# Layer-0 experts ranked by token count on the chip: ten places of 128 slots, six of 64 in pairs

## The chip, the cores and the metric

One core of a Trainium2 chip runs the whole kernel in one launch. The metric is the device time of an execution in microseconds, the median of several runs; a profiled execution gives the trace.

## The reference

A two-layer diffusion block on 512 tokens (256 of context, 256 latent) of width 1024. Each layer has a token mixer (an mLSTM, latent attention and a gated MLP side by side) and then a mixture of 16 experts. Only the experts of layer 0 matter here. A router picks for each token one of four groups and in it two experts, with weights:

```python
combine = einsum('blk,blke->ble', top_w, one_hot(expert_id, 16))
out = zeros_like(h)
for e in range(16):
    hidden = silu(h @ w1[e]) * (h @ w3[e])      # 1024 x 512 each
    out = out + combine[..., e:e+1] * (hidden @ w2[e])   # 512 x 1024
```

All is float32. In layer 0 all 512 tokens go through it, so 1024 pairs of a token and an expert, 64 for an expert on average; in the last layer only the 256 latent tokens.

## The kernel before, in words

`block_kernel` (L1724) runs mixer 0, the layer-0 experts, mixer 1, the layer-1 experts and the last norm. The weights (6.29 MB for an expert, float32) stream from memory once.

`stream_rows` (L1677) makes the plan of the layer-0 weights. It walks the experts 0 to 15; for each it adds the k-steps of w1 and w3 in turn (`("h", e, w)`, eight each; a k-step is a row of 128 x 512, 256 KB), and behind them the eight of w2 of the expert before (`("y", e - 1, q)`). `Pipe.add` (L112) cuts this into units by the tag of the buffer that takes each: FIRST0 (L52) for the first 29 units, then RING0 (L53) round and round, 16 units of 28 rows. There are 221 units. A unit is one DMA on SP's queue (L158), issued as soon as its buffer is free; units 0 to 18 (`PRE0`, 40 rows: both first matrices of experts 0 and 1 and the second of expert 0) are loaded before the router (L1820).

`Pipe.fill` (L162) splits each unit, three items ahead of use, into a rounded half (ACT, L99) and the rest (DVE, a few on POOL, L100), both in the format fp32r. `mm3` (L84) then does three matmuls for each product (L85 to L87), hi x hi, hi x lo and lo x hi.

`route` (L1142) writes the normalized tokens to memory (`h2d`), makes the logits, and ranks each token among those of its expert (`rp`; `pr[:, nt]` holds the counts). Its `weights` (L1241) makes the combine weights `wE` and the largest count `mci`. All of that is small work on DVE.

`moe_rows` (L1340) gives each expert 128 slots. `slots` (L1351) makes one-hot tiles (slot against token) and from them the row index `idx`; `gather` (L1387) is an indirect DMA on POOL that fetches the token rows; `prep` (L1392) transposes them and splits them; `slot_weights` (L1372) brings the combine weight to the slots. The loop over the experts (L1475) issues the gather of e + 3, prepares e + 1, makes slots of e + 4, then does the two first products of e (48 matmuls), SiLU (L1495), the product with the other half (L1498), and the second product of e - 1 (24 matmuls, `second`, L1411), whose result ACT scales and an indirect DMA on POOL adds into `fsum` in memory (L1427). The last two experts (`LATE`) stay on the chip and are added by matmul. At e = 4 (`OVER0`) every engine loads the largest count into a register (L1500) and branches: over 128, a slow loop over all experts would add the tokens beyond (`overflow`, L1316); the profiled execution does not take it.

`moe_chip` (L1531), the experts of layer 1, works in pairs: two experts share a tile of 128 slots, 64 each. Their weights are used unsplit; each product is two matmuls of 64 columns, one for each half of the slots (L1641, L1592), read by `paired` (L1666), which takes a unit of the one and one of the other.

Buffers that matter: `a` (nine: gathered tokens, x, ysb, split tiles), `h` (8), `b2` (6), `w`, `wa`, `e2` (2 each), `t2` (4).

Of the kernel before, what the change touches and what calls it, by code (L numbers as in the profile page):

```python
# [21 lines left out]
P = 128  # L22
D = 1024
KT = 8
# [31 lines left out]
TURN = 8  # L56
OVER0 = 4
EARLY1 = ((0, 1), (14, 15), (16, 17), (), (), (), ())
WHO = ("01010101", "0101")
# [43 lines left out]
class Pipe:  # L103
# [8 lines left out]
    def add(self, key, parts, kt, nk, kind=""):  # L112

        tag = self.tags(len(self.units))
        nk = min(unit_rows(tag), nk)
        u = len(self.units)
        self.units.append((tag, [p[kt * P:(kt + nk) * P] for p in parts], nk))
# [1024 lines left out]
def route(g, l):  # L1142
# [98 lines left out]
    def weights():  # L1241
        r.rk = rk = sm("rk", [P, 5, 16])
        nc.vector.tensor_copy(rk[:, 0:nt + 1], pr[:, 0:nt + 1])
        mc = sm("mc", [P, 1])
        nc.vector.tensor_reduce(mc, rk[:, nt, :], axis=AX.X, op=ALU.max)
        r.mci = g.s([P, 1], I32, "mci")
# [20 lines left out]
        for k, dst in ((0, r.wE), (1, w2)):  # L1267
            nc.vector.tensor_tensor(dst, Ek[:, k, 0:nt].rearrange("p t a b -> p t (a b)"), pw[:, :, k:k + 1].to_broadcast([P, nt, 16]), op=ALU.mult)
        nc.vector.tensor_tensor(r.wE, r.wE, w2, op=ALU.add)
    r.weights = weights  # L1270
    return r
# [44 lines left out]
def overflow(g, l, r, cap, put_tile):  # L1316
# [3 lines left out]
    wt = g.s([P, 4, 16], F32, "ovw")  # L1320
    nc.vector.tensor_scalar(wt[:, 0:nt], r.rk[:, 0:nt], float(cap) - 0.5, None, op0=ALU.is_gt)
    nc.vector.tensor_tensor(wt[:, 0:nt], wt[:, 0:nt], r.wE, op=ALU.mult)
# [16 lines left out]

def moe_rows(g, r, st, cap=P):  # L1340

    nc = g.nc
    nt = r.nt
    n_tok = nt * P
    idx = g.s([P, 16, 1], I32, "idx")
    sw = g.s([P, 16], F32, "sw")
    wp = g.s([P, 4, 16, 3], BF16, "wp")
# [3 lines left out]
    def slots(e):  # L1351
# [3 lines left out]
        for i in range(nt):  # L1355
            oh = g.s([P, P], BF16, "oh")
            ohs.append(oh)
            nc.vector.tensor_scalar(oh, g.iota, r.rp[:, i, e:e + 1], None, op0=ALU.is_equal)
# [4 lines left out]
        if e >= NE - LATE:  # L1363
            tok = g.s([P, 1], F32, "tok")
# [7 lines left out]
    def slot_weights(e, ohs):  # L1372
        pt = g.mm()[:, 0:3]
        for i in range(nt):
            nc.tensor.matmul(pt, ohs[i], wp[:, i, e, :], start=(i == 0), stop=(i == nt - 1))
        nc.vector.tensor_reduce(sw[:, e:e + 1], pt, axis=AX.X, op=ALU.add)

    def weight_planes():

        rest = g.s([P, 4, 16], F32, "rest")  # L1380
        nc.vector.tensor_copy(wp[:, :, :, 0], r.wE)
        nc.vector.tensor_tensor(rest, r.wE, wp[:, :, :, 0], op=ALU.subtract)
        nc.vector.tensor_copy(wp[:, :, :, 1], rest)
        nc.vector.tensor_tensor(wp[:, :, :, 2], rest, wp[:, :, :, 1], op=ALU.subtract)
# [7 lines left out]
    def prep(e):  # L1392
        x = g.t([P, 2, KT, P], F32R, "a", "x")
        for q in range(2):
            pt = g.bank([P, 4, P], "pt")
            for c in range(4):
                k = q * 4 + c
                nc.tensor.transpose(pt[:, c, :], xg[(e // 2) % 2][:, e % 2, k * P:(k + 1) * P], g.ident)
            split_from(g, x[:, 0, q * 4:q * 4 + 4, :], x[:, 1, q * 4:q * 4 + 4, :], pt)
        return x  # L1400

    def turned(G):

        pt = g.bank([P, 4, P], "pt")
        for c in range(4):
            nc.tensor.transpose(pt[:, c, :], G[:, c * P:(c + 1) * P], g.ident)
        gh, gl = [g.t([P, 4, P], F32R, "cz", "gtr") for _ in range(2)]
        split_from(g, gh, gl, pt)
        return gh, gl

    def second(e, gh, gl):  # L1411
        ysb = g.t([P, 2, D], F32R, "a", "yhl") if e in late else g.t([P, D], F32, "a", "ysb")
        for q in range(2):
            py = g.bank([P, 512], "py")
            for kt, nk, raw in st.matrix(("y", e, q), 4):
                for kk in range(nk):
# [9 lines left out]
        if e not in late:  # L1426
            nc.gpsimd.indirect_dma_start(out=g.fsum, out_offset=bass.IndirectOffsetOnAxis(ap=idx[:, e, 0:1], axis=0),  # L1427
                                         in_=ysb, in_offset=None, bounds_check=n_tok - 1, oob_is_err=False, compute_op=ALU.add)
        return last
# [14 lines left out]
    def total(k, e, ps):  # L1444

        y, C = late[e]
        for part in range(2):
            nc.tensor.matmul(ps, y[:, part, k * P:(k + 1) * P], C, start=(e == NE - LATE and part == 0), stop=(e == NE - 1 and part == 1))

# [24 lines left out]
    pend = None  # L1474
    for e in range(NE):  # L1475
        if e + 3 < NE:
            gather(e + 3)
        if e + 1 < NE:
            xs[e + 1] = prep(e + 1)
        if e + 4 < NE:  # L1480
            slot_weights(e + 4, slots(e + 4))
        x = xs.pop(e)
        ph = [g.mm() for _ in range(2)]
        at = [0, 0]
        while min(at) < KT:
            if pend is not None and len(pend) == 2 and sum(at) >= TURN:
                pend = (pend[0],) + turned(pend[1])
            w = st.peek()[2]
# [6 lines left out]
        last = nc.scalar.activation(G, ph[0], AF.Silu)  # L1495
        if e == NE - 1:
            preload(g, last, AF.Sqrt)
        nc.vector.tensor_tensor(G, G, ph[1], op=ALU.mult)  # L1498
        if e == OVER0:
            cnt = nc.values_load(r.mci[0:1, 0:1], min_val=0, max_val=T)  # L1500
            with g.tc.If(cnt > cap):
                def put(i, acc):
                    for q in range(2):
# [4 lines left out]
                        nc.sync.dma_start(rows, acc[q])  # L1508
                overflow(g, 0, r, cap, put)
        if pend is not None:  # L1510
            last = second(*pend)
            if e == NE - LATE:
                fs = load_sums()
        pend = (e, G)
    ps = {k: g.mm() for k in range(4)}
    for k in range(4):
        total(k, NE - 2, ps[k])
    second(pend[0], *turned(pend[1]))
    with g.tc.issue_after(last.ins):
        for k in range(KT):  # L1520
            add_sums(k)
    for k in range(KT):
        if k >= 4:
            ps[k] = g.bank([P, 512], "tot")
            total(k, NE - 2, ps[k])
        total(k, NE - 1, ps[k])
        to_x(k, ps[k], WHO1[k] == "1")
# [149 lines left out]
def stream_rows(g):  # L1677
# [3 lines left out]

    def ys(e):
        for q in range(2):
            st.add_matrix(("y", e, q), [w2_view(g, 0, e, q)], 4)
    for e in range(NE):
        at = [0, 0]
        while min(at) < KT:
            w = 0 if at[0] <= at[1] else 1
            at[w] += st.add(("h", e, w), [(g.e_w1, g.e_w3)[w][0, e]], at[w], KT - at[w])
        if e:  # L1690
            ys(e - 1)
    ys(NE - 1)
    return st
# [30 lines left out]
def block_kernel(ctx, tc, x_t, c_t, vecs, w_ada, w_adt, w_in, w_gk, w_uq2, a_wukv, gws, gbs, w_pa, w_pb, w_pc, w_out,  # L1724
# [56 lines left out]
    g.w4 = const("w4", [P, 4])  # L1781
    nc.gpsimd.iota(g.w4, [[-1, 4]], base=4, channel_multiplier=0, allow_small_or_imprecise_dtypes=True)

    g.mask = [const(f"mask{d}", [P, P], dt=BF16) for d in range(2)]
# [156 lines left out]
```

## Time and profile before

| | |
|---|---|
| median of 3 runs | 1627.12 us (1625.97 to 1627.9) |
| the profiled execution | 1623.76 us |
| its span | 1622.0 us |
| TensorE busy | 1516.7 us, 94% |
| VectorE busy | 1079.6 us, 67% |
| ScalarE busy | 709.6 us, 44% |
| moved by DMA | 358.25 MB, mean 221 GB/s |
| mean granted TensorE clock | 0.974 |

The span runs from the first to the last instruction. The layer-0 experts take the stretch from about 650 to 962 us, the layer-1 experts from about 1360 on. A share of a whole span mixes stages with different limits; the stretch of the change has rows of its own below. A busy TensorE is not TensorE at its peak, since the ends of matmuls are modelled and overlap.

### The profile page before, as it was taken

To read this page: it belongs to the slowest core of one execution; us is meant where nothing else is said; L and a number is where in the kernel's file an instruction comes from. 1 tells how busy PE (TensorE), PEld (TensorE's weight loads), DVE (VectorE), ACT (ScalarE), POOL (GpSimd) and SP (SyncE) were. 2 spreads that over 40 slices of the span, in tenths; PEclk is the share of its full clock that TensorE was granted. 3 is DMA by queue.
4 is the path that set the end of the run, shared out by engine and by line. 5 is a ranking of instruction groups with operands and counts; after the bars stand their busy time and mean duration, and the time that the engine had idled before them with its cause. 6 is when DMAs were issued, how large, how long until landed. Compare 5 with 4: busy or idle time off the path is not lost. (4 is left out here: it accounts for less than half of the span.)

```text
span 1622.0 us, 22586 instructions
## 1 busy us (share of the span) xinstructions
PE 1516.7 (94%) x8283; PEld 1136.6 (70%) x8283; DVE 1079.6 (67%) x2085; ACT 709.6 (44%) x1185; POOL 131.3 (8%) x129
## 2 busy tenths in 40 slices
PE   7899999997999997898979999999999998999997
PEld 5677777686777776676867776886789996453443
DVE  4868996488987655887968977576587675222213
ACT  3335333444422322676867776534566452011011
POOL 1001000003000022211211111010020001000000
PEclk9999999998999999999999999999999999999999
DMA  9615464123477884598999992422236786899995
GB/s 320 209 51 189 156 195 129 40 66 117 148 246 263 276 290 165 185 298 271 357 317 296 367 341 65 124 82 78 65 103 187 254 277 228 320 386 387 386 386 218
DMA packets 180969, 358.25 MB, mean 221 GB/s; under 512 B 13934, under 2 KB 30894, under 8 KB 180592
## 3 DMA queue, kind: packets, MB, share of 16 engines
q1 hardware_dynamic: 173920, 341.10, 62.0%
q0 software_dynamic: 6640, 15.53, 3.6%
q8 instruction: 68, 1.11, 0.3%
q14 instruction: 53, 0.43, 0.1%
q10 hardware_dynamic: 288, 0.07, 0.0%
HBM read 351.77 MB, written 12.60 MB: 225 GB/s over the span
## 5 line engine op out<-in xcount | busy, mean ns | idle before, releaser
L99 ACT ACTIVATE whi<-wraw 128x512 fp32r<-128x512 f32 (+4 forms) x358 | 279.9, 803 | 327.6 <-PE mm L86 220.8
L100 DVE TENSOR_TENSOR wlo<-wraw,whi 128x512 fp32r<-128x512 f32 (+4 forms) x356 | 319.4, 911 | 126.4 <-ACT whi L99 119.1
L85 PE MATMUL mm<-h,whi 128*128 128x512 f32 (+1 forms) x672 | 237.1, 359 | 7.7 <-DVE bt L936 4.0
L86 PE MATMUL mm<-h,whi 128*128 128x512 f32 (+1 forms) x672 | 238.0, 355 | 0.0
L87 PE MATMUL mm<-h,wlo 128*128 128x512 f32 (+1 forms) x672 | 233.3, 352 | 2.1 <-DVE wlo L100 2.1
L85 PEld LDWEIGHTS mm<-h,whi 128*128 128x128 f32 x672 | 129.4, 194 | 31.9 <-DVE bt L936 6.8
L87 PEld LDWEIGHTS mm<-h,wlo 128*128 128x128 f32 x672 | 128.8, 192 | 21.1 <-DVE wlo L100 3.6
L86 PEld LDWEIGHTS mm<-h,whi 128*128 128x128 f32 x672 | 129.6, 193 | 18.6 <-issue 4.4
L100 DVE TENSOR_TENSOR whl<-wraw,whl 128x1024 fp32r<-128x1024 f32 (+1 forms) x110 | 115.0, 1068 | 15.2 <-ACT whl L99 15.2
L1641 PE MATMUL mm<-wraw,x 128*64 128x512 f32 x504 | 121.2, 596 | 0.0
L335 DVE CUSTOM_DVE_ANT_0 adw<-adw,cbc,vec 128x1024 f32<-128x1024 f32 x80 | 102.1, 1280 | 24.6 <-DMA adw<-in_w_adt 24.2
L99 ACT ACTIVATE whl<-wraw 128x1024 fp32r<-128x1024 f32 (+1 forms) x112 | 100.9, 931 | 21.0 <-issue 9.4
L1641 PEld LDWEIGHTS mm<-wraw,x 128*64 128x64 f32 x504 | 36.7, 137 | 67.5 <-issue 62.7
L85 PE MATMUL mm<-by,whi 128*128 128x512 f32 (+1 forms) x192 | 66.6, 347 | 4.5 <-ACT sg L922 4.5
L87 PE MATMUL mm<-by,wlo 128*128 128x512 f32 (+1 forms) x192 | 65.8, 342 | 0.0
L86 PE MATMUL mm<-by,whi 128*128 128x512 f32 (+1 forms) x192 | 65.7, 342 | 0.0
L86 PE MATMUL mm<-wlo,h 128*128 128x512 f32 x160 | 65.7, 410 | 0.0
L85 PE MATMUL mm<-whi,h 128*128 128x512 f32 x160 | 65.2, 411 | 0.1
L335 DVE CUSTOM_DVE_ANT_0 prod<-adw,cbc,vec 128x1024 bf16<-128x1024 f32 x48 | 61.2, 1280 | 6.0 <-DMA adw<-in_w_adt 5.9
L87 PE MATMUL mm<-whi,h 128*128 128x512 f32 x160 | 64.5, 403 | 0.0
L1592 PE MATMUL py<-wraw,gt 128*64 128x512 f32 x256 | 63.8, 598 | 0.7 <-ACT gt L1582 0.7
L85 PE MATMUL mm<-whi,x 128*128 128x512 f32 x128 | 53.0, 415 | 9.0 <-ACT whi L99 8.8
(455 smaller groups left out, 2971.0 us busy)
## 6 DMA issues: line engine op xcount, KB each, us to landing
wraw<-in_e_w SPq DMA_DIRECT2D x278, 512.0 KB, 8.7
wraw<-in_w_in SPq DMA_DIRECT2D x96, 512.0 KB, 3.9
adw<-in_w_adt SPq DMA_DIRECT2D x80, 512.0 KB, 4.2
wraw<-in_e_w SPq DMA_DIRECT2D x33, 1024.0 KB, 13.2
wraw<-in_e_w SPq DMA_DIRECT2D x76, 256.0 KB, 6.7
adw<-in_w_ada SPq DMA_DIRECT2D x8, 1024.0 KB, 12.3
wraw<-in_w_out SPq DMA_DIRECT2D x16, 512.0 KB, 5.7
wraw<-in_w_pb SPq DMA_DIRECT2D x8, 512.0 KB, 3.6
```

The lines of the kernel that those rows point to most:

```text
L85: nc.tensor.matmul(ps, lh, rh, start=first, stop=False)
L86: nc.tensor.matmul(ps, lh, rl, start=False, stop=False)
L87: return nc.tensor.matmul(ps, ll, rh, start=False, stop=last)
L99: g.nc.scalar.activation(hi, src, AF.Copy)
L100: (eng or g.nc.vector).tensor_tensor(lo, src, hi.bitcast(F32), op=ALU.subtract)
L335: g.nc.vector.tensor_tensor_reduce(out=out, in0=raw, in1=g.cbc[:, s, :], scale=1.0, scalar=g.vec[l][:, C_BADA + j:C_BADA + j + 1], op0=ALU ...
L1592: nc.tensor.matmul(py[hs, :], gt[:, k, hs], raws[s][:, kk, :], start=(k == 0), stop=(k == 3))
L1641: nc.tensor.matmul(ph[w][hs, :], x[:, k, hs], raws[s][:, kk, :], start=(k == 0), stop=(k == KT - 1))
```

## The change

Layer 0 gets 16 places instead of 16 experts. Experts 0 and 1 keep places 0 and 1 (`FIXED`); the others are ranked by token count on the chip (`order`, on DVE) and take places 2 to 15, largest first. Places 0 to 9 (`WIDE`) work as before: 128 slots, split weights, three matmuls for a product. Places 10 to 15 work in three pairs of 64 slots with unsplit weights, as layer 1 does. `ORDER` is the order of these 13 steps. `ordered` permutes the ranks (`rP`) and the combine weights (`wP`) into the order of places. SP loads the numbers of the 14 experts at places 2 to 15 into registers, and the transfers of their weights take their addresses from these. A pair's results are added by two scatters, since both experts may have the same token: the first of the lower 64 slots, the second of all 128 with the lower half out of bounds (`upper`). The branch now asks for a count above the place's own capacity, 128 or 64. The plan has 221 units as before, of the same sizes.

```diff
+FIXED = 2
+WIDE = 10
+ORDER = ((0,), (1,), (10, 11), (2,), (3,), (12, 13), (4,), (5,), (14, 15), (6,), (7,), (8,), (9,))
...
     def load_unit(self, u):
-        tag, parts, nk = self.units[u]
+        tag, parts, kt, nk = self.units[u]
+        parts = [(p() if callable(p) else p)[kt * P:(kt + nk) * P] for p in parts]
...
     def weights():
-        nc.vector.tensor_reduce(mc, rk[:, nt, :], axis=AX.X, op=ALU.max)
+        if l == 0:
+            order()
+            nc.vector.tensor_tensor(r.key, rk[:, nt, :], r.cap, op=ALU.subtract)
+            nc.vector.tensor_reduce(mc, r.key, axis=AX.X, op=ALU.max)
+            nc.vector.tensor_scalar(mc, mc, 0.0, None, op0=ALU.max)
...
+        if l == 0:
+            r.wP = sm("wP", [P, 4, NE])
+            ordered(r.wP, r.wE)
+    def order():
+        full = [P, NE, NE]
+        r.key = key = sm("key", [P, NE])
+        nc.vector.scalar_tensor_tensor(key, r.rk[:, nt, :], float(NE), g.tie, op0=ALU.mult, op1=ALU.add)
+        more = g.t([P, 512], F32, "t2", "more")[:, 0:NE * NE].rearrange("p (a b) -> p a b", b=NE)
+        nc.vector.tensor_tensor(more, key[:, None, :].to_broadcast(full), key[:, :, None].to_broadcast(full), op=ALU.is_gt)
+        place = sm("place", [P, NE])
+        nc.vector.tensor_reduce(place, more, axis=AX.X, op=ALU.add)
+        r.at = sm("at", [P, NE, NE])
+        nc.vector.tensor_tensor(r.at, place[:, None, :].to_broadcast(full), g.num[:, :, None].to_broadcast(full), op=ALU.is_equal)
+        who = g.t([P, 512], F32, "t2", "who")[:, 0:NE * NE].rearrange("p (a b) -> p a b", b=NE)
+        nc.vector.tensor_tensor(who, r.at, g.num[:, None, :].to_broadcast(full), op=ALU.mult)
+        whof = sm("whof", [P, NE])
+        nc.vector.tensor_reduce(whof, who, axis=AX.X, op=ALU.add)
+        whoi = g.s([P, NE], I32, "whoi")
+        nc.vector.tensor_copy(whoi, whof)
+        for p in range(FIXED, NE):
+            g.who[p] = nc.values_load(whoi[0:1, p:p + 1], engines=[mybir.EngineType.SP], min_val=0, max_val=NE - 1,
...
+        r.cap = sm("cap", [P, NE])
+        nc.vector.tensor_scalar(r.cap, place, WIDE - 0.5, 64.0, op0=ALU.is_lt, op1=ALU.mult)
+        nc.vector.tensor_scalar(r.cap, r.cap, 64.0, None, op0=ALU.add)
+        r.rP = sm("rP", [P, 4, NE])
+        ordered(r.rP, r.rp)
+    def ordered(dst, src):
+        for i in range(0, nt, 2):
+            full = [P, 2, NE, NE]
+            t = g.t([P, 512], F32, "t2", "ord").rearrange("p (i a b) -> p i a b", a=NE, b=NE)
+            nc.vector.tensor_tensor(t, src[:, i:i + 2, None, :].to_broadcast(full), r.at[:, None, :, :].to_broadcast(full), op=ALU.mult)
+            nc.vector.tensor_reduce(dst[:, i:i + 2, :], t, axis=AX.X, op=ALU.add)
...
     def prep(e):
-        x = g.t([P, 2, KT, P], F32R, "a", "x")
+        x = g.t([P, KT, P], F32, "a", "x") if pair[e] else g.t([P, 2, KT, P], F32R, "a", "x")
...
+    def beside(ps, key, K, x):
+        for kt, nk, raws in paired(st, key, K):
+            for kk in range(nk):
+                k = kt + kk
+                for h, raw in zip(halves, raws):
+                    last = nc.tensor.matmul(ps[h, :], x[:, k, h], raw[:, kk, :], start=(k == 0), stop=(k == K - 1))
+            yield last
...
         if e not in late:
-            nc.gpsimd.indirect_dma_start(out=g.fsum, out_offset=bass.IndirectOffsetOnAxis(ap=idx[:, e, 0:1], axis=0),
+            for h, ix in ((halves[0], idx), (slice(0, P), upper)) if pair[e] else ((slice(0, P), idx),):
+                nc.gpsimd.indirect_dma_start(out=g.fsum, out_offset=bass.IndirectOffsetOnAxis(ap=ix[h, e, 0:1], axis=0),
...
-    for e in range(NE):
+    for e in range(U):
...
+        for w in range(2 if pair[e] else 0):
+            if w:
+                pend = (pend[0],) + turned(*pend)
+            for _ in beside(ph[w], ("h", e, w), KT, x):
+                at[w] = KT
...
             cnt = nc.values_load(r.mci[0:1, 0:1], min_val=0, max_val=T)
-            with g.tc.If(cnt > cap):
+            with g.tc.If(cnt > 0):
...
 def stream_rows(g):
+    def of(m, p, cols=slice(0, DE)):
+        if p < FIXED:
+            return m[0, p][:, cols]
+        return lambda: m[0, ds(g.who[p], 1), :, cols].rearrange("o p f -> p (o f)")
+    def beside(key, srcs, K):
+        kt = 0
+        while kt < K:
+            u = len(st.units)
+            most = min([K - kt] + [unit_rows(st.tags(u + s)) for s in range(2)])
+            for s in range(2):
+                st.add(key + (s,), [srcs[s]], kt, most, "raw")
+            kt += most
...
+    for u, places in enumerate(ORDER):
+        if len(places) == 2:
+            for w, m in enumerate((g.e_w1, g.e_w3)):
+                beside(("h", u, w), [of(m, p) for p in places], KT)
```

## Rows read from the trace of the kernel before

**Rows 1.** Engines by stretch: busy us (records), granted clock, DMA share, GB/s.
```profile
650.00:962.00 312.00, 287.99 (x1362) 226.22 (x1361) 264.40 (x352) 228.15 (x300) 54.69 (x33) 0.97 0.90 304
650.00:670.00 20.00, 14.72 (x83) 10.97 (x82) 19.42 (x30) 12.01 (x17) 11.84 (x7) 0.96 0.43 134
...
730.00:750.00 20.00, 15.27 (x57) 11.82 (x57) 12.84 (x16) 9.65 (x12) 3.48 (x4) 0.84 0.76 262
...
790.00:810.00 20.00, 20.00 (x98) 15.79 (x96) 18.86 (x30) 16.69 (x23) 4.89 (x3) 1.00 1.02 350
...
930.00:950.00 20.00, 20.00 (x93) 16.13 (x92) 18.26 (x21) 16.07 (x21) 1.55 (x1) 1.00 1.04 375
...
1420.00:1440.00 20.00, 20.00 (x107) 10.32 (x105) 4.42 (x13) 2.48 (x4) 0.00 (x0) 1.00 1.05 387
```

**Rows 2.** Timeline of ACT, one expert's SiLU: start, us, wait before.
```profile
681.11 0.60 ACT L1495 ACTIVATE G<-mm 128x512 f32<-128x512 f32 x1 [1.72 <-PE mm L87]
...
739.64 0.60 ACT L1495 ACTIVATE G<-mm 128x512 f32<-128x512 f32 x1 [0.34 <-PE mm L87]
...
767.39 0.60 ACT L1495 ACTIVATE G<-mm 128x512 f32<-128x512 f32 x1 [1.02 <-PE mm L87]
...
892.33 0.60 ACT L1495 ACTIVATE G<-mm 128x512 f32<-128x512 f32 x1 [1.48 <-PE mm L87]
...
948.20 0.60 ACT L1495 ACTIVATE G<-mm 128x512 f32<-128x512 f32 x1 [0.77 <-PE mm L87]
```

**Rows 3.** Branch by line; ACT's waits, 812 to 853; SP's, 650 to 962.
```profile
L1501 PEldq COMPARE_BRANCH  x1: 5777/5777/5777, 739.6 to 739.6; - x1
...
ACT whl L99 <- issue: 6.2, 1, 6.2
ACT whl L99 <- DMA fsum<-ysb,idx: 5.9, 1, 5.9
...
SPq L158 <- DVE wlo L100: 77.1, 66, 6.9
```

**Rows 4.** Groups by line, 1360 to 1622: busy, mean ns, idle before.
```profile
L1641 PE MATMUL mm<-wraw,x 128*64 128x512 f32 x504 | 121.2, 596 | 0.0
L1592 PE MATMUL py<-wraw,gt 128*64 128x512 f32 x256 | 63.8, 598 | 0.7 <-ACT gt L1582 0.7
```

**Rows 5.** Timeline of TensorE: transposes, small products, a paired stretch.
```profile
653.82 1.03 PE L1398 MATMUL pt<-ident,xg 128*128 128x128 f32 x8
...
750.87 0.24 PE L1375 MATMUL mm<-wp,oh 128*128 128x3 bf16 x4
...
1513.76 0.60 PE L1580 MATMUL pt<-ident,G 128*128 128x128 f32 x4
...
1514.29 7.09 PE L1641 MATMUL mm<-wraw,x 128*64 128x512 f32 x32
```

**Rows 6.** DMA queues and issues, 650 to 962; us to landing last.
```profile
q1 hardware_dynamic: 45552, 87.04, 79.2%
q0 software_dynamic: 3859, 7.45, 10.1%
...
fsum<-ysb,idx POOLq DMA_INDIRECT x14, 8.8
```

**Rows 7.** DVE groups of three sizes, layer-0 expert stage and its end.
```profile
L1245 DVE TENSOR_REDUCE mc<-rk 128x1 f32<-128x16 f32 x1 | 0.2, 164 | 0.0
...
L1457 DVE SCALAR_TENSOR_TENSOR xT<-pt,ada,xT 128x256 f32<-128x256 f32 x10 | 4.2, 475 | 0.0
...
L100 DVE TENSOR_TENSOR x<-pt,x 128x512 fp32r<-128x512 f32 x32 | 21.1, 684 | 2.5 <-ACT x L99 2.4
```

**Rows 8.** SP's queue by line: ns min/median/max, first and last start.
```profile
L1500 SPq TENSOR_LOAD <-mci x1: 460/460/460, 643.4 to 643.4; - x1
...
L1500 SPq FUSED_REGOPS  x1: 176/176/176, 644.0 to 644.0; - x1
...
L158 SPq DMA_DIRECT2D wraw<-in_e_w x205: 327/368/2197, 603.1 to 962.0; - x103
```

More of the change, by code (lines that the diff above doesn't have):

```diff
@@ L116, in add @@
         u = len(self.units)
-        self.units.append((tag, [p[kt * P:(kt + nk) * P] for p in parts], nk))
+        self.units.append((tag, parts, kt, nk))
         step = 2 if kind != "raw" else nk
@@ L1344, in moe_rows @@
     n_tok = nt * P
+    U = len(ORDER)
+    pair = [len(p) == 2 for p in ORDER]
+    halves = (slice(0, 64), slice(64, P))
     idx = g.s([P, 16, 1], I32, "idx")
+    upper = g.s([P, 16, 1], I32, "upper")
+    off = g.s([P, 1], F32, "off")
+    nc.vector.memset(off[0:64], 2 * BIG + 256.0)
+    nc.vector.memset(off[64:P], BIG + 256.0)
     sw = g.s([P, 16], F32, "sw")
@@ L1357, in slots @@
             ohs.append(oh)
-            nc.vector.tensor_scalar(oh, g.iota, r.rp[:, i, e:e + 1], None, op0=ALU.is_equal)
+            rank = lambda p: (r.rp if p < FIXED else r.rP)[:, i, p:p + 1]
+            if pair[e]:
+                for h, p in zip(halves, ORDER[e]):
+                    nc.vector.tensor_scalar(oh[:, h], g.iota[:, 0:64], rank(p), None, op0=ALU.is_equal)
+            else:
+                nc.vector.tensor_scalar(oh, g.iota, rank(ORDER[e][0]), None, op0=ALU.is_equal)
             nc.tensor.matmul(pt, oh, g.pln[:, i, :], start=(i == 0), stop=(i == nt - 1))
@@ L1362, in slots @@
         nc.vector.scalar_tensor_tensor(idx[:, e, :], tb[:, 0:1], BIG + 256.0, tb[:, 1:2], op0=ALU.add, op1=ALU.add)
-        if e >= NE - LATE:
+        if pair[e]:
+            nc.vector.scalar_tensor_tensor(upper[:, e, :], tb[:, 0:1], off, tb[:, 1:2], op0=ALU.add, op1=ALU.add)
+        if e >= U - LATE:
             tok = g.s([P, 1], F32, "tok")
@@ L1374, in slot_weights @@
         for i in range(nt):
-            nc.tensor.matmul(pt, ohs[i], wp[:, i, e, :], start=(i == 0), stop=(i == nt - 1))
+            if pair[e]:
+                for h, p in zip(halves, ORDER[e]):
+                    nc.tensor.matmul(pt[h, :], ohs[i][:, h], wp[:, i, p, :], start=(i == 0), stop=(i == nt - 1))
+            else:
+                nc.tensor.matmul(pt, ohs[i], wp[:, i, ORDER[e][0], :], start=(i == 0), stop=(i == nt - 1))
         nc.vector.tensor_reduce(sw[:, e:e + 1], pt, axis=AX.X, op=ALU.add)
@@ L1414, in second @@
             py = g.bank([P, 512], "py")
-            for kt, nk, raw in st.matrix(("y", e, q), 4):
+            if pair[e]:
+                for last in beside(py, ("y", e, q), 4, gh):
+                    pass
+            for kt, nk, raw in () if pair[e] else st.matrix(("y", e, q), 4):
                 for kk in range(nk):
@@ L1447, in total @@
         for part in range(2):
-            nc.tensor.matmul(ps, y[:, part, k * P:(k + 1) * P], C, start=(e == NE - LATE and part == 0), stop=(e == NE - 1 and part == 1))
+            nc.tensor.matmul(ps, y[:, part, k * P:(k + 1) * P], C, start=(e == U - LATE and part == 0), stop=(e == U - 1 and part == 1))
     def to_x(k, ps, by_pool):
@@ L1680, in stream_rows, with ys @@
     st.pool, st.ahead = POOL0, AHEAD0
-    def ys(e):
-        for q in range(2):
[L1684 to L1692, printed above, removed]
+    g.who = {p: p for p in range(FIXED)}
+    def of(m, p, cols=slice(0, DE)):
[10 more added lines that the diff above has]
+            kt += most
+    def ys(u):
+        for q in range(2):
+            srcs = [of(g.e_w2, p, slice(q * 512, (q + 1) * 512)) for p in ORDER[u]]
+            if len(srcs) == 2:
+                beside(("y", u, q), srcs, 4)
+            else:
+                st.add_matrix(("y", u, q), srcs, 4)
+    for u, places in enumerate(ORDER):
+        if len(places) == 2:
+            for w, m in enumerate((g.e_w1, g.e_w3)):
+                beside(("h", u, w), [of(m, p) for p in places], KT)
+        else:
+            at = [0, 0]
+            while min(at) < KT:
+                w = 0 if at[0] <= at[1] else 1
+                at[w] += st.add(("h", u, w), [of((g.e_w1, g.e_w3)[w], places[0])], at[w], KT - at[w])
+        if u:
+            ys(u - 1)
+    ys(len(ORDER) - 1)
     return st
```

57 lines of the change are left out of this document (39 added, 18 removed).

## The prediction

> **What bounds the kernel now.** I read the slices of the page first: the layer-0 expert stage lies at 650 to 962 us, a fifth of the span. Then I tabled the engines over stretches of it [rows 1]. Over the whole stage TensorE is busy 288 of 312 us, VectorE 264, and the DMA engines 0.90 of the time at 304 GB/s. In the last steady stretch, 930 to 950, TensorE has no gap, VectorE is busy 18.3 of 20 us and the DMA share is 1.04 at 375 GB/s. All three run close to their limits, and TensorE is the one without a gap.
>
> One expert's price comes from the times at which its SiLU runs [rows 2]: from 892.33 to 948.20 lie three experts, 18.6 us each, with nothing stalled. From 739.64 to 767.39 it takes 27.8 us, 9 more: the branch on the overflow count stops TensorE's queue there for 5.8 us [rows 3], and the granted clock of that stretch is 0.84 [rows 1]. Two further stalls sit between 812 and 853: ACT, about to write a split tile, waits 5.9 and 6.2 us, once by name for a scatter to land [rows 3].
>
> Transfers wait for buffers and not the other way round: SP's queue stood 77.1 us behind the DVE splits of one kind alone [rows 3]. So before the change the weights arrive early enough.
>
> **The change part by part.**
>
> *Pairs on TensorE.* Layer 1 already runs its experts as two tiles of 64 slots, so the price is in the trace. There are 760 records for 384 products, two records each [rows 4], and a stretch without a stall does 32 records in 7.09 us, 0.222 us each [rows 5]. A pair has 48 products (32 for w1 and w3, 16 for w2), 96 records, 21.3 us. To it come eight transposes on the way in (1.03), four of G (0.60) and 12 small products for slots and weights (four take 0.24, so 0.7) [rows 5]: 23.6 us against 2 x 18.6 = 37.2. Each pair saves 13.6 us, three save 41. The weight splits of the six experts go from ACT and DVE too; that is worth nothing by itself while TensorE has no gap, it only makes room.
>
> *Transfers.* No byte of weight is saved. In the stage the hardware queue moved 87.04 MB and the software queue, gathers and scatters, 7.45 MB [rows 6]. An expert is 24 rows of 256 KB, 6.29 MB, and with 0.53 MB of gather and scatter (7.45 over the 14 scatters) 6.82 MB. At the 375 GB/s of the best stretch [rows 1] that is 18.2 us, 0.76 us for a row. ORDER sets a pair after each two wide experts, three times: such a block is four experts, 72.8 us of transfers against 37.2 + 23.6 = 60.8 us of TensorE. Here the transfers are the slower of the two, by 12 us a block.
>
> What stands against it is the lead. The first pair begins near 693 (expert 1's SiLU at 681.1 [rows 2], 6 us of the later start worked out below, 5.5 for the 24 second products of expert 0, at (18.6 - 1.03 - 0.60 - 0.5) / 72 = 0.229 us each, the three subtracted prices being those of the pair above). By then the buffers hold 38 rows beyond the two preloaded experts: ten single rows of FIRST0 and one turn of RING0, 28. Later the lead cannot grow past 28 rows, one turn of the ring. The last first-product row of the third pair is row 224, so 186 remain: 141 us, to 834, and a few us for the last to land. TensorE needs from 693: three times 16.6 us (64 records and the small work), four wide first products of 13, four wide second products of 5.5, two paired ones of 7.1, and 9 for the branch, 147 us, to 840. That is a dead heat. But around the branch the full ring holds transfers back for about 10 us (48 rows are used in 48 us, 63 could land, and the lead is full before), and from there to the end of the third pair's second products TensorE wants 40 rows in 26 us that take 30. So TensorE waits about 12 us in or after the third pair. I charge half, 6 us: the two stalls of 12 us that were there before leave transfers time to catch up, so one hides part of the other. Both ends, 0 and 24 (at 350 GB/s, the stretch 790 to 810 [rows 1], an expert takes 19.5 us and the lag grows by 12), stay for the range.
>
> The Trainium skill, page "DMA: Bandwidth & Descriptors", section "Specifications", puts the HBM limit of one core at about 358 GB/s; by it an expert would take 19.0 us and the lag would grow by 8 us. The trace speaks against it: 387 GB/s at 1420 to 1440 [rows 1].
>
> *Ranking.* order() and both calls of ordered() add to DVE five operations on 256 elements (0.475 each by the nearest row), eight on 512 (0.684) and about seven on 16 (0.164) [rows 7]: 2.4 + 5.5 + 1.1 = 9 us. They stand before the slot weights, for which TensorE waits ahead of expert 0. In 650 to 670 DVE is busy 19.4 of 20 us [rows 1], so little hides them there; in the wait for the first gather just before, DVE has some 3 us free. I take 6 us, with 0 and 9 as ends.
>
> *Register loads.* SP must now wait for the ranking and load 14 registers: 0.46 us each and 0.18 of register work, with gaps about 0.9 [rows 8], 12.6 us. The count for the branch was loaded at 643.4 [rows 8]; the ranking's part that SP needs is some 2.7 us longer at most, so the registers are there near 657. Behind them in SP's queue stand all weight loads from unit 19 on. Cover: the two fixed experts and the second product of expert 0 are preloaded, so the first of these rows is wanted near 693, and 36 us at 375 GB/s are 47 rows, more than the 38 that fit. Cost 0; without the cover it is about 14 us.
>
> *Register addresses.* 198 of 221 transfers (places 0 and 1 need none: 23) now have an address worked out on SP. An issue is 0.368 us [rows 8]; the trace has no such transfer. Nearest is one register operation, 0.176 us [rows 8]: I take two, 0.7 us per transfer, 142 us in a stage of 270, hidden. The lower end is no addition (an addition to an issue cannot gain); the upper end is the third rival below.
>
> *Gather, scatter, branch.* 13 gathers instead of 16, and 14 scatters as before (eight wide, two for each pair). A pair's second scatter adds into the same sums and may wait for the first: 8.8 us to landing [rows 6], with the next gather behind it in POOL's queue; that is issued three units ahead and can stand it. The tile ysb is held that much longer; what this may cost is in the second rival, between 0 and 18 us. The branch at unit 4 stays. The token counts that the reference's router gives in this layer are 108, 103, 91, 91, 84, 80, 65, 60, 58, 52, 46, 42, 37, 37, 36, 34, with 46 and 34 for the fixed experts 0 and 1; so the largest of a pair is 58, under 64, and the branch is not taken.
>
> **Sum.** 41 saved, less 6 at the start, less 6 of lag: 29 us. The profiled execution took 1623.76 us (span 1622.0 and 1.76 around it), 3.4 below the median of 1627.12; it would become 1594.8, and the median **1598**.
>
> **Rivals.** *TensorE alone sets the pace*: transfers keep up and the two scatter stalls, 12 us, vanish, since the pairs use fewer "a" tiles for splits; 41 + 12 less 0 to 6, so 1574 to 1580. For it speaks the 387 GB/s of layer 1; against it that there no scatters ran beside. Chance 0.18.
>
> *Given back to transfers and scatters*: the rate stays at 350 GB/s (another 12 us of lag), or each pair's second scatter costs a stall of about 6 us like those between 812 and 853, three times, 18 us, or both: 1610 to 1628. Chance 0.20, of it 0.05 within 0.2% of before. The limit on the page "DMA: Bandwidth & Descriptors" of the Trainium skill would give 1606; a rate held that low has 0.04 of the 0.20, given the 387 [rows 1].
>
> *SP's issue becomes the bound* (slower): if each register address costs 1.17 us more, SP needs 1.54 x 198 = 305 us from 657 and ends at 962 as before; at 1.5 us more it ends at 1027, 65 us later: 1692. That would take eight operations like the 0.176 us one. Chance 0.10.
>
> *It does not do what it says*: the branch is taken for a count above 64. It would load 4 x 16 x 24 rows of 256 KB, 403 MB, at 387 GB/s over 1000 us. The counts exclude it; chance 0.02 with everything else of that sort.
>
> **How the numbers follow.** The forecast, 1586 to 1606, has 0.50; the four others 0.18, 0.20, 0.10, 0.02. Faster by over 0.2% (3.3 us, about what a measurement of this kernel can tell from no change) is 0.50 + 0.18 + 0.15 = 0.83, the same 0.05, slower 0.12. The range 1575 to 1626 leaves out the slower cases and a little at either end.
>
> **What would show it.** Right: SiLU to SiLU about 24 us over a pair and its neighbours' second products, 18.6 between wide ones; SP's first register-address transfer near 657; expert 1's SiLU near 687; DMA share near 1.04 for most of 690 to 870; TensorE idle on weight transfers only around the third pair; the stage's end some 29 us earlier. Wrong: no idle time on transfers at all (first rival); ACT waiting for a scatter after each pair (second); gaps over 30 us between SiLUs with SP always issuing (third); a granted clock below 1.00 in the pairs.

## The result, and the profile after

The changed kernel takes **1606.71 us** (median of 4 runs, 1604.34 to 1609.53) against 1626.61 (1625.97 to 1627.9) of the kernel before in the same session: ratio 0.987, 95% interval 0.9852 to 0.9889. That is 20 us faster, where 29 were forecast. The profiled execution took 1607.61 us with a span of 1605.9; before these were 1623.76 and 1622.0.

The two profiled spans lie 16.1 us apart, and all of that gain lies in the layer-0 expert stage. As its length I take the time from SP's first write of token rows (`h2d`) to layer 1's first SiLU; this leaves out what the router and the mixer did earlier or later in one execution. Before: 630.62 to 1373.21, 742.6 us. After:

```profile
632.78 0.34 SPq L1204 DMA_DIRECT2D h2d<-htok  x1
...
1357.48 0.60 ACT L1740 ACTIVATE G<-mm 128x512 f32<-128x512 f32 x1 [8.81 <-PE mm L1738]
```

Those are two rows of the timeline, SP's and ScalarE's: 724.7 us, **17.9 less**. From that SiLU to the end of the span it takes 248.4 us, before 248.8: layer 1 is as it was.

The same stretches as in [rows 1], after the change (engines' busy us, granted clock, DMA share, GB/s):

```profile
650.00:962.00 312.00, 278.30 (x1238) 177.29 (x1239) 185.32 (x282) 158.68 (x202) 53.60 (x35) 0.95 0.91 321
650.00:670.00 20.00, 12.90 (x74) 10.27 (x74) 17.34 (x62) 7.51 (x10) 7.11 (x6) 0.66 0.57 180
730.00:750.00 20.00, 19.93 (x95) 11.24 (x93) 9.79 (x17) 7.91 (x10) 2.73 (x2) 1.00 1.02 356
790.00:810.00 20.00, 17.98 (x79) 11.30 (x76) 9.85 (x16) 9.59 (x12) 3.02 (x2) 0.91 1.05 392
930.00:950.00 20.00, 19.23 (x86) 14.81 (x85) 16.60 (x18) 14.36 (x18) 1.56 (x1) 1.00 1.04 371
```

VectorE and ScalarE have become light: 185 and 159 us of 312, against 264 and 228. TensorE now has gaps at 790 to 810, where it had none, with the DMA share at 1.05. A finer table of the stage's start and its length shows what has changed places (same columns):

```profile
650.00:660.00 10.00, 3.54 (x22) 3.39 (x23) 8.47 (x21) 3.43 (x6) 1.26 (x1) 0.67 0.81 264
660.00:670.00 10.00, 9.36 (x58) 6.87 (x55) 8.86 (x41) 4.08 (x4) 5.85 (x5) 0.65 0.33 96
670.00:680.00 10.00, 8.02 (x38) 5.95 (x38) 8.15 (x4) 4.88 (x6) 5.59 (x2) 1.00 0.14 42
680.00:690.00 10.00, 10.00 (x59) 8.26 (x58) 10.00 (x15) 8.47 (x10) 1.90 (x1) 1.00 0.18 35
690.00:700.00 10.00, 10.00 (x49) 7.32 (x48) 8.02 (x20) 4.38 (x6) 0.00 (x0) 1.00 0.47 159
...
695.00:950.00 255.00, 231.01 (x1006) 140.48 (x1005) 134.02 (x184) 124.36 (x161) 36.71 (x23) 0.97 0.99 353
```

For 30 us, 660 to 690, the transfers all but stop (96, 42 and 35 GB/s), at a time when weights should be stocked up for the first pair. From 695 to 950 they run at a share of 0.99, and TensorE stands still for 24 of the 255 us: 2 of them directly for weights, 17 for splits of ScalarE and VectorE, 5 at the branch. The waits of SP's queue in 655 to 700 name the stop (engine and line, what was waited for, us in total, times, longest):

```profile
SPq L162 <- DVE wlo L103: 30.2, 1, 30.2
SPq L162 <- PE mm L1495: 7.2, 1, 7.2
```

One wait of 30.2 us: after the ten single rows (650.5 to 657.7) SP stands in front of unit 29, the first of the ring, whose `w` buffer the last split of expert 1 sets free. The next transfers go out at 688.80. Nothing behind it in SP's queue can pass. Later the waits in 690 to 950 are on the other side:

```profile
ACT whi L102 <- DMA wraw<-in_e_w: 25.4, 6, 11.0
...
POOL fsum L1519 <- DMA fsum<-ysb,idx: 18.3, 3, 6.6
...
PEld mm L1495 <- DMA wraw<-in_e_w: 8.0, 14, 2.5
...
PE py L88 <- ACTq L1598: 4.7, 1, 4.7
...
PE mm L88 <- ACT whi L102: 4.3, 3, 2.0
...
ACT ysb L1511 <- DMA fsum<-ysb,upper: 3.9, 1, 3.9
PE mm L89 <- DVE wlo L103: 3.9, 6, 1.1
...
PE mm L1495 <- DMA wraw<-in_e_w: 1.9, 2, 1.6
```

ScalarE waits 25.4 us for weights to split, and TensorE for such splits; TensorE's weight loads wait 8.0 us for weights themselves. The second scatter of each pair waits for the first on GpSimd's queue (18.3 in all); the branch still stops TensorE for 4.7 us. In place of the 12 us in which ACT waited in 812 to 853 [rows 3] it waits 5.5 us for second scatters (3.9 and 1.6). The SiLUs that answer to [rows 2]:

```profile
678.19 0.60 ACT L1592 ACTIVATE G<-mm 128x512 f32<-128x512 f32 x1 [3.32 <-PE mm L90]
690.93 0.60 ACT L1592 ACTIVATE G<-mm 128x512 f32<-128x512 f32 x1 [1.43 <-PE mm L90]
707.25 0.60 ACT L1592 ACTIVATE G<-mm 128x512 f32<-128x512 f32 x1 [6.32 <-PE mm L1495]
740.34 0.60 ACT L1592 ACTIVATE G<-mm 128x512 f32<-128x512 f32 x1 [2.13 <-PE mm L90]
...
788.21 0.60 ACT L1592 ACTIVATE G<-mm 128x512 f32<-128x512 f32 x1 [6.44 <-PE mm L1495]
...
866.45 0.60 ACT L1592 ACTIVATE G<-mm 128x512 f32<-128x512 f32 x1 [2.98 <-PE mm L1495]
```

The first pair's SiLU comes 16 us after expert 1's, and then 33 us pass to the next. The last two rows are the SiLUs of the second and third pair: 81 and 78 us from pair to pair. And the new work on SP's queue, as in [rows 8] (ns min/median/max, first and last start):

```profile
L1302 SPq TENSOR_LOAD <-whoi x14: 267/272/462, 649.8 to 923.3; - x14
...
L162 SPq DMA_DIRECT2D wraw<-in_e_w x202: 332/373/2902, 650.5 to 946.8; - x101
L162 SPq FUSED_REGOPS  x198: 37/46/56, 650.3 to 946.1; - x198
L162 SPq MOVE wraw<-in_e_w x198: 29/29/38, 650.4 to 946.8; - x198
```

A register load is 0.27 us, and an address from a register costs 0.046 + 0.029 us beside an issue of 0.373. SP spends 0.45 us on such a transfer.

### The profile page after: what moved, and what is told of

It is laid out like the page before. It is cut to its first block, busy times and chain, and to the rows that moved or that the text cites. A ratio compares the mean times of both kernels' runs of the same rounds, so it can differ in the third digit from the quotient of the medians.

```text
span 1605.9 us, 22277 instructions
## 1 busy us (share of the span) xinstructions
PE 1490.1 (93%) x8091; PEld 1073.9 (67%) x8091; DVE 990.6 (62%) x1995; ACT 629.3 (39%) x1074; POOL 127.3 (8%) x127
## 5 line engine op out<-in xcount | busy, mean ns | idle before, releaser
L102 ACT ACTIVATE whi<-wraw 128x512 fp32r<-128x512 f32 (+3 forms) x313 | 240.8, 791 | 351.7 <-PE mm L89 221.0
L103 DVE TENSOR_TENSOR wlo<-wraw,whi 128x512 fp32r<-128x512 f32 (+2 forms) x311 | 276.8, 906 | 132.1 <-ACT whi L102 128.5
L103 DVE TENSOR_TENSOR whl<-wraw,whl 128x1024 fp32r<-128x1024 f32 (+1 forms) x65 | 74.1, 1145 | 6.4 <-ACT whl L102 6.3
L102 ACT ACTIVATE whl<-wraw 128x1024 fp32r<-128x1024 f32 (+1 forms) x67 | 63.9, 963 | 8.7 <-DMA wraw<-in_e_w 4.3
L1743 DVE TENSOR_TENSOR G<-G,mm 128x512 f32<-128x512 f32 x8 | 5.5, 688 | 73.6 <-PE mm L1738 67.2
```

The lines of the kernel that those rows point to most:

```text
L102: g.nc.scalar.activation(hi, src, AF.Copy)
L103: (eng or g.nc.vector).tensor_tensor(lo, src, hi.bitcast(F32), op=ALU.subtract)
```

## The experiments

The theory at first, A: the transfers bind from 700 on, and the time is lost to the stop of SP's queue at 658 to 688, which leaves a lead of ten rows instead of 38. The rivals: the register loads, the ranking, the pairs' second scatters, or TensorE itself. (The expectations of e1_lead and e4_half call the last of these theory B; from e5_static_lead on, theory B is another, set out there.) The table gives the median, the ratio to the runs of before in the same session with its interval, and the stage as defined above from the profiled execution. That is one execution each and can lie some us off the median: those of e2_static, e7_lead_slots and e9_order are the fastest of their four, those of e11_lead_nopool and e12_two_late the slowest.

| kernel | us | ratio [95%] | stage, us |
|---|---|---|---|
| before | | 1 | 742.6 |
| changed | 1606.71 | 0.9870 [0.9852, 0.9889] | 724.7 |
| e1_lead | 1595.75 | 0.9795 [0.9768, 0.9823] | 713.2 |
| e2_static | 1593.37 | 0.9786 [0.9766, 0.9806] | 710.4 |
| e3_norank | 1589.3 | 0.9751 [0.9720, 0.9781] | 711.1 |
| e4_half | 1578.62 | 0.9689 [0.9655, 0.9722] | 700.9 |
| e5_static_lead | 1590.56 | 0.9783 [0.9758, 0.9807] | 710.6 |
| e6_lead_before | 1631.66 | 1.0023 [1.0005, 1.0042] | 750.9 |
| e7_lead_slots | 1597.65 | 0.9828 [0.9807, 0.9849] | 713.9 |
| e8_one_scatter | 1605.12 | 0.9867 [0.9848, 0.9886] | 724.8 |
| e9_order | 1597.19 | 0.9827 [0.9803, 0.9850] | 713.0 |
| e10_lead_two | 1622.65 | 0.9976 [0.9959, 0.9994] | 742.2 |
| e11_lead_nopool | 1594.47 | 0.9790 [0.9769, 0.9811] | 715.1 |
| e12_two_late | 1599.91 | 0.9831 [0.9798, 0.9863] | 718.8 |

### Another order of the buffers (e1_lead)

```diff
-FIRST0 = ['b2']*4+['a']+['h']*4+['a']*2+['wa']*2+['w']*2+['h']*4+['b2']*4+['e2']*2+['t2']*4
-RING0 = ['w']*2+['b2']*4+['wa']*2+['h']*8
+FIRST0 = ['w']*2+['wa']*2+['h']*4+['a']*3+['h']*4+['b2']*4+['b2']*2+['e2']*2+['t2']*4+['w']*2+['wa']*2+['h']*4
+RING0 = ['h']*4+['b2']*4+['w']*2+['wa']*2+['h']*4
```

> The buffers of the plan are renamed so that the tiles wanted first for the third unit (w, wa, four h) are those that expert 0 frees, not expert 1: SP no longer stands 30 us behind expert 1's last split. Nothing else changes. Theory A (transfers set the stage's end; the queue lies idle between 665 and 695 and is saturated from there to 950): up to 16 more rows of 0.7 us land in the idle stretch, 8 to 12 us less than the changed kernel's 1606.7, so 1595 to 1599. Theory B (TensorE and the late start set it): no change, within 3 us of 1606.7.

Measured: 1595.75 us, 11.5 us off the stage. The buffers that come up first again are now those that expert 0 frees. The transfers no longer stop from 670 on, though a hole is left at 680 to 690 (columns as above):

```profile
660.00:670.00 10.00, 6.06 (x36) 4.21 (x35) 8.76 (x31) 2.99 (x5) 4.89 (x4) 0.50 0.48 148
670.00:680.00 10.00, 10.00 (x43) 7.98 (x42) 5.64 (x8) 6.49 (x7) 5.42 (x3) 0.95 1.00 354
680.00:690.00 10.00, 8.89 (x55) 7.17 (x54) 9.77 (x13) 8.27 (x10) 4.43 (x2) 1.00 0.28 86
```

That bears theory A out: 11.5 us hang on a list of buffer names.

### The same order in the kernel before (e6_lead_before)

The same two lines in the kernel before.

> Control: the kernel of before with nothing but the new buffer order. Theory: before, TensorE bound the stage (253 us busy of 272), so what an earlier transfer gains is waited for elsewhere: 1622 to 1629 us (ratio 0.996 to 1.001). Rival: the order of the buffers is worth its 11 us in any kernel of this shape, and the change only happened to meet it: 1613 to 1618 us.

Measured: ratio 1.0023, a little slower, outside the expected range on the side away from the rival. So the order of the buffers is not worth its 11 us in every kernel of this shape. Why not, this run does not tell. The expectation puts it down to TensorE, which binds there. But there was no stop to take away either: the kernel before has constant addresses, its transfers stand in an order of the compiler's (next section), and in 655 to 700 SP's longest wait in it is 11.3 us:

```profile
SPq L158 <- POOL whl L100: 13.4, 2, 11.3
```

### Constant addresses, and no ranking (e2_static, e3_norank)

```diff
+RANKED = [0, 1, 9, 7, 10, 11, 5, 8, 6, 4, 13, 14, 15, 2, 3, 12]
...
-        for p in range(FIXED, NE):
-            g.who[p] = nc.values_load(whoi[0:1, p:p + 1], ...)
...
-        if p < FIXED:
-            return m[0, p][:, cols]
-        return lambda: m[0, ds(g.who[p], 1), :, cols].rearrange("o p f -> p (o f)")
+        return m[0, RANKED[p]][:, cols]
```

The ranking stays, and only SP's addresses no longer come from it. e3_norank also takes out `order`, `ordered` and their 17 instructions on VectorE, and indexes ranks and weights by the same list.

> The ranking is computed as before, but the weights' addresses are constants for these inputs: no register loads and no register addresses. Theory A: the 198 moves of 0.029 us and 14 loads of 0.27 us lie where SP waits for buffers anyway, so 1604 to 1608. Rival (the register path on SP delays the transfers): 8 us or more less, 1599 or below.

> No ranking on the chip: places, addresses, ranks and weights are constants of these inputs, 9 us of DVE work and the register loads are gone. Theory A: the first product comes about 8 us earlier (655 instead of 663), expert 1's last split with it, and the transfers behind it, so 8 us less: 1597 to 1601. If the start does not matter since transfers fill what follows anyway: 1604 to 1608.

Measured: 1593.37, 13 us under the changed kernel where theory A expected nothing, and 1589.3. Two lessons. The ranking costs nothing that these runs can tell: without it the first product starts at 649.65 us instead of 659.94, and the stage is no shorter (711.1 against 710.4; the two ratios' intervals overlap). But the register addresses cost something that theory A did not have. With constant addresses transfers start at 638, and SP's waits in 655 to 700 hold no block of 30 us:

```profile
SPq L163 <- DVE wlo L104: 14.8, 5, 8.9
SPq L163 <- POOL wlo L104: 11.2, 1, 11.2
```

The buffers are the same and so is the work that frees them. What differs, beside the loads themselves, is the order of SP's queue. In the built programs the transfers behind the ten single rows stand so (units in the order of issue; 29 and 30 take the `w` buffers, 31 to 34 `b2`, 35 and 36 `wa`, 37 to 44 `h`):

```
kernel before:       31 32 37 38 39 40 35 36 29 30 41 42 43 33 44 34
changed kernel:      29 30 31 32 33 34 35 36 37 38 39 40 41 42 43 44
constant addresses:  31 32 37 38 39 40 35 36 29 30 41 42 43 44 33 34
```

With constant addresses the compiler moves the two transfers that will wait longest behind eight others (the next expectation says six), and in the kernel before it had done the same. With addresses from registers it leaves the order in which the kernel writes them.

### Is it that order? (e5_static_lead, e9_order)

Theory B: the register addresses cost their 13 us by fixing the order of the queue, so that they and the buffer order of e1_lead are one and the same stall. e5_static_lead has both edits. e9_order is the changed kernel, registers, ranking and buffers and all, with the order of sixteen transfers written by hand:

```diff
         while self.loaded < min(n, len(self.units)):
+            for u in self.early.get(self.loaded, ()):
+                self.load_unit(u)
             self.load_unit(self.loaded)
...
+    st.early = {29: (31, 32, 37, 38, 39, 40, 35, 36), 33: (41, 42, 43, 44)}
```

> Constant addresses (no register loads) and the new order of the buffers in one kernel. Theory B: in the programs themselves the constant addresses let the compiler move the two rows that wait for the w buffer (unit 29, the first of the ring) behind six other loads, and loads with an address from a register stand in the order in which the kernel writes them; so both edits take away one and the same stall of SP's queue and their gains don't add: 1590 to 1595 us, no more than 5 below the run with the new buffer order alone (1595.75) nor below the one with constant addresses alone (1593.37). Rival: the register loads cost their 13 us by themselves, beside the stall: 1581 to 1584 us. In the trace under B: the transfers' share over 690-950 is 0.99 or more, as it was.

> The changed kernel with its register loads and its buffers as they are; only the order in which the kernel writes sixteen transfers is another: units 31, 32 and 35 to 40 are issued ahead of units 29 and 30 (the two that wait for the w buffers), and 41 to 44 ahead of 33 and 34, which is the order on SP's queue that the compiler made of the kernel with constant addresses. Theory B (the 13 us of the constant addresses are this order): 1592 to 1597 us, and no wait of SP over 15 us in 655-700. Rival (the register loads and their 10 us later first transfer cost them): 1603 to 1608 us. Between: 1598 to 1602 us would share it out by where the time falls.

Measured: 1590.56, so the gains don't add (the stage: 710.6, against 710.4 and 713.2 with one edit alone). By the ratios, constant addresses gain 14 us with the old order of the buffers (0.9870 to 0.9786) and 2 with the new one (0.9795 to 0.9783). And 1597.19 for the order alone, just beyond the upper edge of what B expected; the stage is 11.7 us shorter than that of the changed kernel. SP's waits in 655 to 700 are now those of the constant addresses:

```profile
SPq L165 <- DVE wlo L103: 14.2, 5, 8.7
SPq L165 <- POOL wlo L103: 11.4, 1, 11.4
```

By these executions 11.7 of the 14.3 us of stage that the register addresses cost are the order. Both executions without the stop are the fastest of their runs, though; by the ratios of all runs the order alone gains 7 us of 14, give or take 5. So the order is shown to cost, and since constant addresses gain only 2 us where the new buffers have taken the stop away, it is most of the 14. What the rest is stays open; it may be the later first transfer (646.7 against 638.1).

### What the transfers still take (e4_half, e8_one_scatter)

```diff
...
-            for s in range(2):
+            for s in range(1):
                 st.add(key + (s,), [srcs[s]], kt, most, "raw")
```

In e4_half a pair's products take the first expert's weights for both halves, so 72 of 384 rows are not moved.

> Each pair loads the weights of its first expert only and uses them for both halves (the second expert's own weights are left out): 72 of 384 rows are not moved, TensorE's work is the same. Theory A: the transfers no longer bind, TensorE does; 25 us less, 1577 to 1585. Theory B: no change beyond 5 us.

Measured: 1578.62 (2 runs), 23.8 us off the stage with TensorE's instructions all there. The transfers bind the changed kernel. In e8_one_scatter the pair's second scatter is gone.

```diff
-            for h, ix in ((halves[0], idx), (slice(0, P), upper)) if pair[e] else ((slice(0, P), idx),):
+            for h, ix in ((halves[0], idx),) if pair[e] else ((slice(0, P), idx),):
```

> The second scatter of each pair is left out, and with it the adding of the upper 64 slots' rows; all else as in the changed kernel. Theory: the pairs' second scatters wait for the first (18.3 us on GpSimd's queue) but TensorE and the transfers don't wait for them: 1604 to 1608 us, as the changed kernel. Rival: they stand on the path with 6 us each: 1588 to 1592 us.

Measured: 1605.12, the stage 724.8 against 724.7. The 18.3 us for which a second scatter waits on GpSimd's queue cost nothing.

### An earlier first product (e7_lead_slots)

```diff
-    weight_planes()
-    for e in range(4):
+    weight_planes(0, FIXED, r.wE)
+    for e in range(2):
...
+        if e == 0:
+            rest_of_start()
```

`rest_of_start` holds both `ordered`, the planes of places 2 to 15 and the slots, gathers and slot weights of experts 2 and 3.

> The new buffer order, and the ranks and weights of places 2 to 15 put in order (eight instructions of 0.68 us), with the slot weights of experts 2 to 4, only behind expert 0's gate: the first two experts take their numbers unordered. Theory: the first product comes at 655 to 658 us instead of 663, and since the transfers bind from 700 on only what of that lets loads start earlier is kept: 2 to 6 us below the run with the buffer order alone, 1590 to 1594 us. Rival (the start lies on the path at full length): 1586 to 1589 us. Third: the gathers of the first pair come late instead, and the time is 1595 us or more.

Measured: 1597.65. The first product comes at 657.68, as expected, and nothing of it is kept: expert 1's SiLU is at 691.42 (e1_lead: 691.69). Expert 0's first products, 14.7 us in e1_lead (664.08 to 678.77), take 20.3 us here (657.68 to 677.95). In them VectorE is busy 18.2 us, and TensorE waits for its splits and GpSimd's:

```profile
657.68:677.95 20.27, 15.43 (x72) 11.40 (x72) 18.18 (x34) 8.69 (x10) 10.28 (x5) 0.78 0.62 217
```

```profile
PE mm L89 <- DVE whl L103: 2.6, 1, 2.6
```

The edit did less than it says, though. The kernel writes the ordering behind expert 0's gate, but in the program that ran all eight of its instructions stand ahead of the first product; these are the first and the last of them:

```profile
648.33 0.68 DVE L1312 TENSOR_TENSOR ord<-rp,at 128x512 f32<-128x512 f32 x1
...
653.17 0.67 DVE L1313 TENSOR_REDUCE wP<-ord 128x32 f32<-128x512 f32 x1
```

What it took away is that the slot weights of experts 0 and 1 wait for them. What a start without the ordering is worth, with these buffers and addresses from registers, no run shows.

The third theory's number came true, but not its reason: the first pair's SiLU is no later (709.24, e1_lead 709.50).

### Two pairs instead of three (e10_lead_two, e12_two_late)

```diff
-ORDER = ((0,), (1,), (10, 11), (2,), (3,), (12, 13), (4,), (5,), (14, 15), (6,), (7,), (8,), (9,))
+ORDER = ((0,), (1,), (10,), (11,), (2,), (3,), (12, 13), (4,), (5,), (14, 15), (6,), (7,), (8,), (9,))
```

Both on top of the new buffer order; e12_two_late splits up the last pair, (14, 15), instead of the first.

> The new buffer order, and two pairs in place of three: the experts of places 10 and 11 run as single ones of 128 slots with split weights. The same bytes are moved; TensorE works one pair's saving longer (2 x 18.6 less 23.6, 13.6 us) and the vector engines split two experts more. Theory (transfers bind from 700 on; TensorE has 255 less 235 us to spare): 1595 to 1601 us, no more than 5 above the run with the buffer order alone (1595.75). Rival (what TensorE saves is still kept in full): 1608 to 1611 us.

> The new buffer order and two pairs, as in the run before, but the first two pairs stay and the last one (places 14 and 15) runs as two single experts. Same bytes, same TensorE and vector work as that run (1622.65 us). There, the transfers ran at 266 GB/s over 700-790, where SP waited 47.5 us for splits, against 325 GB/s with the first pair in its place: raw rows of a pair come free by the products alone. Theory C (the first pair was missed because it keeps the transfers running while TensorE and the splits catch up): 1597 to 1607 us, with 700-790 at 310 GB/s or more. Rival (a pair is worth its 27 us wherever it stands): 1618 to 1627 us.

Measured: 1622.65 without the first pair, 29 us of stage lost, twice the 13.6 us that a pair saves on TensorE; neither reading expected that. Without the last pair 1599.91, 5.6 us of stage. The same work and the same bytes differ by 23 us by where the pair stands. The stretch 700 to 790, without the first pair and then without the last:

```profile
700.00:790.00 90.00, 74.89 (x320) 57.52 (x319) 63.21 (x94) 52.73 (x68) 12.77 (x9) 0.91 0.79 266
```

```profile
700.00:790.00 90.00, 83.25 (x397) 48.43 (x395) 42.38 (x72) 38.56 (x54) 13.88 (x11) 0.96 0.93 323
```

and SP's waits in it, in the same two kernels:

```profile
SPq L162 <- DVE whl L103: 29.3, 14, 9.9
SPq L162 <- DVE wlo L103: 18.2, 13, 5.4
```

```profile
SPq L162 <- DVE wlo L103: 3.6, 4, 2.3
SPq L162 <- DVE whl L103: 3.3, 4, 1.5
```

A split row's buffer comes free when its split is done, a pair's when its products are. With six single experts in a row the transfers go at the pace of the splits, 266 GB/s, before TensorE's stock has built up. The single experts alone do not do that: the kernel before, which has no others (and constant addresses), moves 310 GB/s in this stretch, and 268 with the new buffer order (e6_lead_before):

```profile
700.00:790.00 90.00, 81.55 (x391) 64.41 (x391) 74.00 (x106) 65.45 (x85) 15.04 (x11) 0.96 0.90 310
```

```profile
700.00:790.00 90.00, 77.19 (x345) 59.60 (x344) 65.91 (x96) 57.60 (x75) 13.22 (x10) 0.91 0.80 268
```

So by these runs it takes both, single experts and the new order; two pairs with the old order were not run. At 266 instead of 323 for 90 us 5.1 MB are missing by 790, which at 366 GB/s (790 to 880, without the last pair) is an estimated 14 us. The transfers, which bind from then on, never make it good; what makes up the other 9 of the 23 us I have not traced.

### GpSimd's splits (e11_lead_nopool)

```diff
-POOL0 = (4,5,7,10)
+POOL0 = ()
```

> The new buffer order, and the four splits of the stage's start that GpSimd takes given to the vector engines. While GpSimd worked on its splits (666 to 676 us), VectorE's of 128x1024 took 2.28 us, 1.22 us afterwards; so 3 or 4 instructions more at 1.22 us against 4 shorter by 1.06: buffers come free within 1 us of the same time. Theory: 1593 to 1597 us, as with the buffer order alone. Rival (VectorE and ScalarE are the bound at the start): 1598 to 1604 us.

Measured: 1594.47, the same as e1_lead.

## Why the prediction was right, and where not

The sign and the mechanism were right: TensorE's saving, partly taken back by transfers. The median lies 9 us above the forecast of 1598, just past the forecast's own 1586 to 1606 and inside the outer range, 1575 to 1626. What the sum did not have is the stop of SP's queue, about 11 us. The rest of it comes out near the measured time, in part by luck, for several of its terms were off, on either side.

- **Pairs save 41 on TensorE.** With a part of the transfers gone (e4_half) the stage is 41.7 us shorter than before. That the sizes agree so closely is partly chance, for SP's queue still stands in that run (two waits of 14 us in 655 to 700 in place of one of 30), and ScalarE still waits 5.9 us for a scatter.
- **375 GB/s.** Where the transfers are full it held: 371 GB/s at 930 to 950, 392 at 790 to 810. Behind the branch it did not (198 at 770 to 780), and the mean of 695 to 950 is 353. The page "DMA: Bandwidth & Descriptors" of the Trainium skill, section "Specifications", has 358 GB/s as the limit; by the 392 of this trace that does not bind here.
- **A lead of 38 rows by 693.** This is the step that failed. Ten rows were out by 657.7 and the next transfers left at 688.80. I had taken the transfers to be free to fill every buffer, from SP's wait of 77.1 us [rows 3] that I read as "early enough". That order was the compiler's own, made for constant addresses; with addresses from registers the kernel's order stands, and its first ring unit waits for expert 1's last split. Cost: 11.5 us of stage by e1_lead (12 by the ratios), 11.7 by e9_order (7 by the ratios).
- **A lag of 6 us, from the third pair on.** TensorE and ScalarE waited for transfers from the first pair on. With the lead restored (e1_lead) the stage is 29.4 us shorter than before, 12 less than the 41 or so of TensorE: what the sum charged in all, though not by its terms.
- **Ranking, 6 us at the start.** The 512-wide instructions took 0.68 us and the 256-wide 0.41 to 0.43 (0.475 taken). The first product came at 662.98, 11 us later than before, 2 of them from ahead of the stage: 9 us, the upper end given. Worth nothing in the end that the runs can tell: a first product 10 us earlier did not shorten the stage (e3_norank).
- **Register loads, 12.6 us and hidden.** A load took 0.27 us instead of 0.9, and all but two stand far down the queue (714 to 923), so the first transfer left at 650.5 and not at 657. The claim that the register path costs nothing was wrong all the same, for the most part through the order it fixes.
- **Register addresses, 0.7 us.** 0.45, the issue included. SP's issue as the bound, 1692 us, is out: its extra work is 0.075 us for a transfer.
- **Second scatters, 0 to 18 us.** They wait 18.3 us and cost 0 (e8_one_scatter).
- **The signs.** Expert 1's SiLU was to come near 687: it came at 690.93. From pair to pair it took 81 and 78 us, more than the 72.8 of the transfers in the sum. The DMA share was to be near 1.04 from 690: from 710 to 950 it was 1.02, with 0.54 behind the branch (770 to 780). The clock was not below 1.00 in the pairs but in the start (0.66 at 650 to 670).

The best version run is the changed kernel with the new buffer order, 1595.75 us (ratio to before 0.9795), 1594.47 without GpSimd's splits, which is the same.

## What to carry to other kernels

When transfers take their addresses from registers, look at their order on the issuing queue: the compiler may no longer move the ones that wait behind the ones that could go, so write first what will be free first. A saving on one engine is worth what the stage's next limit leaves of it (here 18 to 29 of 41 us), and the head start built before the limit takes over is part of the price. Steps that use buffers raw and steps that hold them through a split are not alike to the transfers, and where they stand can be worth more than their number (23 us here, with the new order of the buffers).

## What the runs showed of the hardware

An address from a register costs SP 75 ns (46 + 29) on top of an issue; a register load took 0.27 to 0.29 us, the first one 0.46.

VectorE's split of 128x1024 took twice as long while GpSimd worked on its own, and GpSimd's took 2.4 to 3.4 us. First VectorE, then GpSimd, by timeline:

```profile
668.76 4.55 DVE L103 TENSOR_TENSOR whl<-wraw,whl 128x1024 fp32r<-128x1024 f32 x2
673.23 4.57 DVE L103 TENSOR_TENSOR wlo<-wraw,whi 128x1024 fp32r<-128x1024 f32 x2
...
681.28 1.23 DVE L103 TENSOR_TENSOR whl<-wraw,whl 128x1024 fp32r<-128x1024 f32 x1
```

```profile
669.63 2.60 POOL L103 TENSOR_TENSOR wlo<-wraw,whi 128x1024 fp32r<-128x1024 f32 x1
672.20 3.40 POOL L103 TENSOR_TENSOR whl<-wraw,whl 128x1024 fp32r<-128x1024 f32 x1
```

Two in 4.55 us, 2.28 each, against 1.23; with GpSimd's splits taken away (e11_lead_nopool) all of VectorE's at 664 to 679 took 1.22 or 1.23. The page "SBUF — State Buffer" of the Trainium skill, section "SBUF: two separate sides", says that a VectorE instruction with two inputs in SBUF and a GpSimd instruction that reads SBUF shut each other out. The traces agree: in e1_lead a split of GpSimd's ends at 676.86, and the one that VectorE starts in the middle of it, at 675.77, ends 1.08 us after that. Three splits given away thus cost VectorE about what it would need for them itself, and the kernel's time does not change.
